# Last groups of a down projection in order of token tiles, the first token tile loaded ahead of a norm's weights, and one power on GpSimd at the beginning

## The chip, the cores and the metric

The kernel runs on one core of one Trainium2 chip. The metric is the device time of one launch in microseconds (us). Engines are named as the profile names them: PE (TensorE), PEld (its weight loads), DVE (VectorE), ACT (ScalarE), POOL (GpSimd) and SP (SyncE, which issues all DMAs of this kernel). Lines are named L275 and the like, by the kernel before.

## The reference, cut to what matters

One decoder layer on x of 512 tokens by 1024 columns, in float32:

```
x = x + 1/2 * SwiGLU_1(RMSNorm(x))
h = RMSNorm(x);  [q | k | v | r | k_r | v_r | c] = h @ W_in
mix = concat(DilatedAttn(QKNorm(q), QKNorm(k), v), RWKV7(r, k_r, v_r, c))
x = x + mix @ W_out
x = x + 1/2 * SwiGLU_2(RMSNorm(x))

SwiGLU(h) = (silu(h @ w_gate) * (h @ w_up)) @ w_down      # 1024 -> 2816 -> 1024
RMSNorm(x) = x * rsqrt(mean(x * x) + 1e-6) * gain
```

## The kernel before

**Tiles.** The 512 tokens are four tiles of 128 (tile 0 to tile 3), the 1024 columns of x two halves of 512 (c = 0, 1). Every float32 product is made as three matmuls of halves of the numbers (`mm3`: high by high, high by low, low by high). So each weight and each transposed x is split into a high part, which ACT casts, and a low part, which DVE or POOL subtracts.

**Stages.** FFN 1 (gate and up projections, then the down projection), the mixing part (W_in, attention, RWKV-7), the W_out projection, FFN 2. The kernel is written with a tile library that orders the instructions of each engine by when they should be ready, in favour of those written first; instructions marked `keep_in_program_order` keep their place. Buffers come from pools with a fixed number of slots; a tile that finds no free slot waits until everything that touches the older one is done.

**The down projection** (`down`) works by a scheme with seven products, m1 to m7, in place of eight: the rows are split in two halves (r = 0 for tiles 0 and 1, r = 1 for tiles 2 and 3), the columns in two, and the 22 blocks of the inner dimension are 11 groups of two. Each product has two accumulators in PSUM (t = 0, 1). `add(acc, t, r, c, sign)` on DVE (L275) adds accumulator t to columns c of tile 2r + t. The last three products are m4, m2 and m6: m4 goes to column half 0 of all four tiles, m2 to both halves of tiles 2 and 3, m6 to half 1 of tiles 2 and 3. Their last three groups (8, 9 and 10) are held back, and `finish(i, m, t)` issues them for one accumulator: nine matmuls of 512 columns. So tile t is complete after m4 of t, and tile 2 + t after m4, m2 and m6 of t.

**The norm that follows.** In FFN 1 a complete tile goes to `done1`, which stores it to DRAM (L471) and calls `norm_T`: the sum of squares of the half that came last (ACT, L96), the scale (POOL, a multiply and add in L115 and a power of -1/2 in L116), the product by scale and gain (DVE, L118, into the tile `xn`, a pool of two slots), and a function, returned, that transposes eight blocks on PE (L125, into two PSUM tiles of the tag "tp", which has two slots) and splits the result into high (ACT, L130) and low (DVE, L131). The transposes are kept in their place of the program. What `down` returns is `hook`, the transposes that are still to be issued; `proj_into` puts them into the first projection of the mixing part, which works on the token columns in two halves of 256 (tiles 0 and 1, then tiles 2 and 3). In FFN 2 nothing follows: `done` returns None, and finished pieces are stored to the output (L277).

Before the change the order is: m4 of t = 0, 1, m2 of t = 0, 1, m6 of t = 0, 1. The transposes of tile 0 stand after m2 of t = 0, those of tile 1 after m2 of t = 1, and those of tiles 2 and 3 are left to `hook`.

**The beginning.** SP's queue holds, in this order, the row of the norm's weights (`row`), tile 0 of x, the identity for transposes, tile 1 of x, then the first two gate and up weights. PE spreads the row over the partitions by matmuls with a row of ones (L457, `one` set on POOL), into two PSUM tiles, `g1`, which DVE multiplies by in L118.

Of the kernel before, what the change touches and what calls it, by code (L numbers as in the profile page):

```python
# [14 lines left out]
ALU = mybir.AluOpType  # L15
# [6 lines left out]
S = 512  # L22
NT = S // P
# [19 lines left out]
def tile_layer(ctx: ExitStack, tc: tile.TileContext, I, out):  # L43
    nc = tc.nc
    V, A, G, T, Q = nc.vector, nc.scalar, nc.gpsimd, nc.tensor, nc.sync
# [10 lines left out]
    nhalf = cpool.tile([P, 16], F32, name="nhalf")[:, 0:8]  # L56
    vec = cpool.tile([P, NV + 2], F32, name="vec")
    fill = spool.tile([P, 24], F32, tag="fill", bufs=1, name="fill")
    G.memset(fill, 0.0)
    G.memset(nhalf, -0.5)  # L60

    def weights(src, width, name, extra=None, lo_eng=None):
        raw = wpool.tile([P, D], F32, tag="wraw", bufs=3, name=f"raw_{name}")
        Q.dma_start(out=raw, in_=src)
        wp = extra or wpool
        hi = wp.tile([P, D], F32R, tag="whi", bufs=2, name=f"hi_{name}")
        lo = wp.tile([P, D], F32R, tag="wlo", bufs=2, name=f"lo_{name}")
        A.copy(out=hi, in_=raw)  # L68
        (lo_eng or V).tensor_tensor(out=lo, in0=raw, in1=hi.bitcast(F32), op=ALU.subtract)  # L69
        return hi.rearrange("p (a b) -> p a b", b=width), lo.rearrange("p (a b) -> p a b", b=width)  # L70
# [8 lines left out]
    def new_xT(name, pool=tpool):  # L79
        return [[pool.tile([P, 4, S], F32R, tag="xT", name=f"{name}{kh}{p}") for p in "hl"] for kh in range(2)]  # L80

    state = {}

    def gain_tile(name):
        g = npool.tile([P, D], F32, tag="gain", bufs=1, name=f"gain_{name}")
        Q.dma_start(out=g, in_=I[name].broadcast_to([P, D]))
        return g[:, 0:S], g[:, S:D]

    def sumsq(x, h, dump, name, eng=None):

        xh = x[:, h * S:(h + 1) * S]
        ss = spool.tile([P, 1], F32, tag="ss", name=f"ss{name}{h}")
        if eng is V:
            V.tensor_tensor_reduce(out=dump, in0=xh, in1=xh, op0=ALU.mult, op1=ALU.add, scale=1.0, scalar=0.0, accum_out=ss)
        else:
            A.activation(out=dump, in_=xh, func=AF.Square, accum_out=ss)  # L96
        return ss

    def guard(ss, name):
        ms = spool.tile([P, 1], F32, tag="ms", bufs=8, name=f"ms{name}")  # L100
        G.tensor_scalar(out=ms, in0=ss, scalar1=1.0 / D, scalar2=EPS, op0=ALU.mult, op1=ALU.add)
        return ms
# [131 lines left out]
    def down(n, U, VV, LL, x, ptile, xp, extra, sd, s17, done, dump, store):  # L234
# [35 lines left out]
        final = set()  # L270

        def add(acc, t, r, c, sign):
            tt = 2 * r + t
            xs = x[tt][:, c * S:(c + 1) * S]
            V.scalar_tensor_tensor(out=xs, in0=acc[t], scalar=0.5 * sign, in1=xs, op0=ALU.mult, op1=ALU.add)  # L275
            if (tt, c) in final and store:
                Q.dma_start(out=store[tt][:, c * S:(c + 1) * S], in_=xs)  # L277
# [27 lines left out]
        ms = [None] * NT  # L305
# [56 lines left out]
        def finish(i, m, t):  # L362
            for g, z in held:
                prod(m, g, *z[i], ts=(t,))

        nxt = [None] * NT
        final.update((tt, c) for tt in range(NT) for c in range(2))
        for t in range(2):
            finish(0, m4, t)
            add(m4, t, 0, 0, 1)  # L370
            nxt[t] = done(t, ms[t])
        final.difference_update([(2, 0), (3, 0), (2, 1), (3, 1)])
        for t in range(2):
            add(m4, t, 1, 0, 1)
        for t in range(2):
            finish(1, m2, t)
            final.add((2 + t, 0))
            add(m2, t, 1, 0, 1)
            add(m2, t, 1, 1, -1)
            if dump:  # L380
                ms[2 + t] = guard(sumsq(x[2 + t], 0, dump(), f"d{n}{2 + t}"), f"d{n}{2 + t}"), 1
            if nxt[t]:
                nxt[t]()
                state.pop('pin', None)
        for t in range(2):
            finish(2, m6, t)
            final.add((2 + t, 1))
            add(m6, t, 1, 1, 1)
            nxt[2 + t] = done(2 + t, ms[2 + t])
        return nxt[2:]  # L390

    def ffn(n, xT, x, hpool, ptile, xp, extra, hook, done, w0, store):
        U, VV, LL, big = [], [], [], []
# [39 lines left out]
    def psum_tiles(c, n, bufs=6):  # L433
        pm = c.enter_context(tc.tile_pool(name=f"pm{n}", bufs=bufs, space=PSUM, reuse_waits="tile"))
        pt = c.enter_context(tc.tile_pool(name=f"pt{n}", bufs=2, space=PSUM, reuse_waits="tile"))
        state['tp'] = lambda shape, tag, name: (pm if tag == "mm" else pt).tile(shape, F32, tag=tag, name=name)
        return state['tp']
# [3 lines left out]
    with ExitStack() as c:  # L441
        xpool = c.enter_context(tc.tile_pool(name="x1", bufs=1, reuse_waits="tile"))
        hpool = c.enter_context(tc.tile_pool(name="h1", bufs=1, reuse_waits="tile"))
        extra = c.enter_context(tc.tile_pool(name="e1", bufs=1, reuse_waits="tile"))
        ptile = psum_tiles(c, 1)
        x1 = [xpool.tile([P, D], F32, name=f"x1_{tt}") for tt in range(NT)]
        xT = new_xT("xa")
        one = spool.tile([1, P], F32, tag="ao", bufs=2, name="one")
        G.memset(one, 1.0)
        row = npool.tile([1, D], F32, tag="gain", bufs=1, name="row")  # L450
        Q.dma_start(out=row, in_=I['ffn1_norm'])
        Q.dma_start(out=x1[0], in_=I['x'][0])
        Q.dma_start(out=ident, in_=I['cst'][:, C_ID:C_ID + P])
        Q.dma_start(out=x1[1], in_=I['x'][1])
        g1 = [ptile([P, S], "mm", f"g1{h}") for h in range(2)]
        for h in range(2):
            T.matmul(g1[h], one, row[:, h * S:(h + 1) * S], start=True, stop=True)  # L457
        for tt in range(2):
            norm_T(x1[tt], g1, xT, tt, "a", tag="tp" if tt == 0 else "mm")()
        w0 = [weights(I['ffn1_w_gu'][0, gu], P, f"gu1_0_{gu}", lo_eng=G) for gu in range(2)]  # L460
        e = state['e']
        for tt in range(2, NT):
            Q.dma_start(out=x1[tt], in_=I['x'][tt])
        with tc.issue_after(e[0].ins), tc.issue_after(e[1].ins):
            hook = [norm_T(x1[tt], g1, xT, tt, "a") for tt in range(2, NT)]

        def done1(tt, ms):
            if tt == 0:
                state['g'] = gain_tile('mix_norm')
                state['xT'] = new_xT("xb")  # L470
            Q.dma_start(out=xd[tt], in_=x1[tt])  # L471
            return norm_T(x1[tt], state['g'], state['xT'], tt, "b", ms)

        hook = ffn(1, xT, x1, hpool, ptile, tpool, extra, hook, done1, w0, None)
# [807 lines left out]
```

## Time and profile before

| | us |
|---|---|
| three runs | 1110.94, 1110.76, 1106.01 (median 1110.76) |
| profiled execution, own time | 1105.09 |
| its span, first to last instruction | 1103.3 |
| PE busy | 1070.1 (97%) |
| DVE, ACT, POOL busy | 677.4, 447.6, 140.5 |

The profile's times count from the start of the span, which is 1.79 us shorter than the execution's own time. PE is busy in almost every slice, so a gain has to come from a stretch in which PE stands, and a loss from one in which it is made to. FFN 1 passes to the mixing part at about 350 to 375 us; the down projection of FFN 2 ends the span.

### The profile page before, as it was taken

How to read it: one execution, taken by the hardware profiler on the slowest of the kernel's cores; microseconds unless marked ns; L12 is line 12 of the kernel's file. 1: busy time of each engine (PE TensorE's matmuls, PEld its weight loads, DVE VectorE, ACT ScalarE, POOL GpSimd, SP SyncE). 2: the span in 40 equal slices, each digit the busy share in tenths (PEclk: the TensorE clock that was granted, in tenths of full speed). 3: DMA queues.
4: the chain of work that ended last, by engine and by line, in shares of the span. 5: the costliest groups of instructions: out<-in, count | busy, mean ns of one | idle time of the engine just before them, and what ended most of it. 6: DMA issues, size and time to landing. Idle time of an engine off the chain costs nothing.

```text
span 1103.3 us, 14413 instructions
## 1 busy us (share of the span) xinstructions
PE 1070.1 (97%) x5380; PEld 896.0 (81%) x5380; DVE 677.4 (61%) x1169; ACT 447.6 (41%) x720; POOL 140.5 (13%) x185
## 2 busy tenths in 40 slices
PE   7999999999999999998899999999999999999998
PEld 6888888888888877777788898788888888888887
DVE  5555464557875735695478468645454655557865
ACT  3332222335654557523343544434332322236652
POOL 3000000000000456203242221212000000000000
PEclk9999999999999999998999999999999999999999
DMA  6556655667556614542321201333566566566663
GB/s 213 181 184 226 227 180 195 225 217 246 189 186 222 200 59 106 153 134 77 105 75 51 86 30 29 129 101 115 194 232 203 181 217 213 199 232 210 212 206 123
DMA packets 84536, 181.14 MB, mean 164 GB/s; under 512 B 23889, under 2 KB 29265, under 8 KB 84466
## 3 DMA queue, kind: packets, MB, share of 16 engines
q1 hardware_dynamic: 84466, 180.22, 50.2%
q8 instruction: 42, 0.69, 0.3%
q14 instruction: 28, 0.23, 0.1%
HBM read 140.87 MB, written 38.27 MB: 162 GB/s over the span
## 4 chain that ended last, share of the span: by engine, by line
PE 79%; DVE 9%; ACT 4%; POOL 3%; DMA 3%; issue 2%; SPq 0%; ACTq 0%; POOLq 0%; DVEq 0%
PE gu L77 14%; PE gu L73 14%; PE gu L76 14%; PE m L76 5%; PE m L77 5%; PE m L73 5%; PE in L77 2%; PE in L76 2%; PE in L73 2%; DMA raw_d<-sd 1%; PE aa L1065 1%; PE cn L1108 1%; DVE pr L867 1%; PE cx L1091 1%; PE acco L76 1%
## 5 line engine op out<-in xcount | busy, mean ns | idle before, releaser
L68 ACT CAST hi_gu<-raw_gu 128x1024 fp32r<-128x1024 f32 x88 | 92.8, 1054 | 271.4 <-PE gu L76 252.3
L69 DVE TENSOR_TENSOR lo_gu<-raw_gu,hi_gu 128x1024 fp32r<-128x1024 f32 x84 | 102.5, 1220 | 49.9 <-ACT hi_gu L68 49.9
L405 DVE TENSOR_TENSOR sg<-gu,sg 128x512 f32<-128x512 f32 x44 | 30.3, 688 | 68.4 <-PE gu L77 67.6
L76 PE MATMUL gu<-xc0l,hi_gu 128*128 128x512 f32 (+1 forms) x184 | 70.0, 380 | 1.6 <-DVE xc0l L131 1.6
L73 PE MATMUL gu<-xa0h,hi_gu 128*128 128x512 f32 (+1 forms) x184 | 70.7, 384 | 0.7 <-ACT xa0h L130 0.7
L76 PE MATMUL gu<-xa0l,hi_gu 128*128 128x512 f32 (+1 forms) x184 | 70.5, 383 | 0.4 <-DVE xa0l L131 0.4
L77 PE MATMUL gu<-xa0h,lo_gu 128*128 128x512 f32 (+1 forms) x184 | 70.4, 383 | 0.0
L73 PE MATMUL gu<-xc0h,hi_gu 128*128 128x512 f32 (+1 forms) x184 | 70.0, 380 | 0.0
L73 PE MATMUL gu<-xa1h,hi_gu 128*128 128x512 f32 (+1 forms) x184 | 70.0, 380 | 0.0
L73 PE MATMUL gu<-xc1h,hi_gu 128*128 128x512 f32 (+1 forms) x184 | 70.0, 380 | 0.0
L77 PE MATMUL gu<-xc1h,lo_gu 128*128 128x512 f32 (+1 forms) x184 | 69.9, 380 | 0.0
L76 PE MATMUL gu<-xc1l,hi_gu 128*128 128x512 f32 (+1 forms) x184 | 69.9, 380 | 0.0
L76 PE MATMUL gu<-xa1l,hi_gu 128*128 128x512 f32 (+1 forms) x184 | 69.9, 380 | 0.0
L77 PE MATMUL gu<-xc0h,lo_gu 128*128 128x512 f32 (+1 forms) x184 | 69.9, 380 | 0.0
L77 PE MATMUL gu<-xa1h,lo_gu 128*128 128x512 f32 (+1 forms) x184 | 69.9, 380 | 0.0
L259 DVE TENSOR_TENSOR lo_d<-raw_d,hi_d 128x1024 fp32r<-128x1024 f32 x39 | 47.6, 1224 | 17.7 <-ACT hi_d L258 17.5
L76 PE MATMUL m<-lo_d,v 128*128 128x512 f32 x148 | 57.7, 390 | 0.2 <-DVE lo_d L259 0.2
L73 PE MATMUL m<-hi_d,v 128*128 128x512 f32 x148 | 57.7, 390 | 0.0
L77 PE MATMUL m<-hi_d,l 128*128 128x512 f32 x140 | 54.5, 389 | 0.0
L259 DVE TENSOR_TENSOR w_d<-raw_d,w_d 128x1024 fp32r<-128x1024 f32 x35 | 42.7, 1222 | 16.1 <-ACT w_d L258 16.0
L231 ACT CAST v<-u 128x512 fp32r<-128x512 f32 (+1 forms) x58 | 33.0, 570 | 45.5 <-PE m L76 45.4
L73 PE MATMUL m<-w_d,v 128*128 128x512 f32 x132 | 51.3, 389 | 0.0
(388 smaller groups left out, 2651.6 us busy)
## 6 DMA issues: line engine op xcount, KB each, us to landing
raw_gu<-in_ffn_w_gu SPq DMA_DIRECT2D x88, 512.0 KB, 4.1
raw_d<-sd SPq DMA_DIRECT2D x66, 256.0 KB, 3.5
raw_in<-in_w_in SPq DMA_DIRECT2D x28, 512.0 KB, 3.7
ra<-in_ffn_w_down SPq DMA_DIRECT2D x22, 512.0 KB, 3.5
rb<-in_ffn_w_down SPq DMA_DIRECT2D x22, 512.0 KB, 5.3
sd<-s SPq DMA_DIRECT2D x22, 512.0 KB, 5.2
s<-ra SPq DMA_DIRECT2D x22, 512.0 KB, 6.0
raw_d<-in_ffn_w_down SPq DMA_DIRECT2D x44, 256.0 KB, 3.3
```

The source lines that it names most:

```text
L68: A.copy(out=hi, in_=raw)
L69: (lo_eng or V).tensor_tensor(out=lo, in0=raw, in1=hi.bitcast(F32), op=ALU.subtract)
L73: first = T.matmul(ps, lh, rh, start=start, stop=False)
L76: T.matmul(ps, lh, rl, start=False, stop=False)
L77: T.matmul(ps, ll, rh, start=False, stop=stop)
L231: A.copy(out=hi, in_=src)
L259: V.tensor_tensor(out=lo, in0=raw, in1=hi.bitcast(F32), op=ALU.subtract)
L405: V.tensor_tensor(out=sg, in0=ps[1], in1=sg, op=ALU.mult)
L867: V.tensor_tensor(out=pr[:, :n1, :n2], in0=au[:, i + 1:, i:i + 1].broadcast_to([P, n1, n2]), in1=tu[:, i:i + 1, :n2].broadcast_to([P, n1, ...
L1065: T.matmul(ps[:, c], bk[:, j, c], xr[:, j, c, 2 * h:2 * h + 2], start=True, stop=True)
L1091: T.matmul(px[:, j, h], xr[:, j, c, 2 * h:2 * h + 2].rearrange("p a b -> p (a b)"), sv[:, j, h, c, :], start=True, stop=True)
L1108: T.matmul(pn[:, j, h], kr[:, j, c, 2 * h:2 * h + 2].rearrange("p a b -> p (a b)"), sv[:, j, h, c, :], start=True, stop=True)
```

## The change

Three parts. In the last groups of `down`, everything of t = 0 is issued first (m4, m2, m6), then everything of t = 1; so the tiles are complete in the order 0, 2, 1, 3. The functions with the transposes go into a list, `late`, from which `turned(n)` issues the oldest until n are left: those of tiles 0 and 2 after m2 of t = 1, those of tile 1 after m6 of t = 1; those of tile 3 alone are returned as `hook`. At the beginning, tile 0 of x is put ahead of the row of weights in SP's queue. And POOL does one power, of a tile of ones, before anything else but two memsets.

```diff
-    G.memset(fill, 0.0)
+    G.memset(fill, 1.0)
     G.memset(nhalf, -0.5)
+    G.tensor_tensor(out=fill[:, 0:8], in0=fill[:, 8:16], in1=nhalf, op=ALU.pow)
...
         nxt = [None] * NT
-        final.update((tt, c) for tt in range(NT) for c in range(2))
+        late = []
+
+        def closed(tt, c):
+
+            if store:
+                Q.dma_start(out=store[tt][:, c * S:(c + 1) * S], in_=x[tt][:, c * S:(c + 1) * S])
+
+        def turned(n):
+            while len(late) > n:
+                f = late.pop(0)
+                if f:
+                    f()
+                    state.pop('pin', None)
+
         for t in range(2):
             finish(0, m4, t)
             add(m4, t, 0, 0, 1)
-            nxt[t] = done(t, ms[t])
-        final.difference_update([(2, 0), (3, 0), (2, 1), (3, 1)])
-        for t in range(2):
+            closed(t, 0)
+            late.append(done(t, ms[t]))
             add(m4, t, 1, 0, 1)
-        for t in range(2):
             finish(1, m2, t)
-            final.add((2 + t, 0))
+            turned(2 - t)
             add(m2, t, 1, 0, 1)
+            closed(2 + t, 0)
             add(m2, t, 1, 1, -1)
             if dump:
                 ms[2 + t] = guard(sumsq(x[2 + t], 0, dump(), f"d{n}{2 + t}"), f"d{n}{2 + t}"), 1
-            if nxt[t]:
-                nxt[t]()
-                state.pop('pin', None)
-        for t in range(2):
             finish(2, m6, t)
-            final.add((2 + t, 1))
+            turned(1)
             add(m6, t, 1, 1, 1)
-            nxt[2 + t] = done(2 + t, ms[2 + t])
-        return nxt[2:]
+            closed(2 + t, 1)
+            late.append(done(2 + t, ms[2 + t]))
+        turned(1)
+        return late
...
+        Q.dma_start(out=x1[0], in_=I['x'][0])
         Q.dma_start(out=row, in_=I['ffn1_norm'])
-        Q.dma_start(out=x1[0], in_=I['x'][0])
```

## Rows read from the trace of the kernel before

**Rows 1.** Waits of PE from 345 to 382 us: total, times, longest.
```profile
PE pTb L125 <- DVE xb0l L131: 1.5, 2, 1.2
```
**Rows 2.** Timeline of PE, FFN 1 to mixing: start, duration, instruction, idle before.
```profile
355.69 0.39 PE L73 MATMUL m<-hi_d,v 128*128 128x512 f32 x1
...
357.74 1.04 PE L125 MATMUL pTb<-ident,xnb 128*128 128x128 f32 x8
358.53 0.47 PE L73 MATMUL m<-hi_d,v 128*128 128x512 f32 x1
...
362.96 0.66 PE L125 MATMUL pTb<-ident,xnb 128*128 128x128 f32 x4 [1.23 <-DVE xb0l L131]
...
367.27 0.27 PE L76 MATMUL in<-xb0l,hi_in 128*128 128x256 f32 x1
...
372.80 1.25 PE L125 MATMUL pTb<-ident,xnb 128*128 128x128 f32 x8 [0.31 <-DVE xb0l L131]
```
**Rows 3.** Timeline of DVE, the same stretch.
```profile
356.42 1.42 DVE L118 SCALAR_TENSOR_TENSOR xnb<-x,rsb,gain_mix_norm 128x512 f32<-128x512 f32 x2 [1.32 <-POOL rsb L116]
...
362.23 0.68 DVE L131 TENSOR_TENSOR xb0l<-pTb,xb0h 128x512 fp32r<-128x512 f32 x1
```
**Rows 4.** Timeline of ACT, the same stretch.
```profile
354.60 0.63 ACT L96 ACTIVATE xnb<-x 128x512 f32<-128x512 f32 x1 [2.87 <-DVE x L275]
...
359.16 0.57 ACT L130 CAST xb0h<-pTb 128x512 fp32r<-128x512 f32 x1
...
360.36 1.03 ACT L68 CAST hi_in<-raw_in 128x1024 fp32r<-128x1024 f32 x1
```
**Rows 5.** Timeline of POOL, the same stretch.
```profile
355.49 0.26 POOL L115 TENSOR_SCALAR rsb<-ssb,msd 128x1 f32<-128x1 f32 x1 [61.55 <-ACT xnb L96]
355.84 0.55 POOL L116 TENSOR_TENSOR rsb<-rsb,nhalf 128x1 f32<-128x1 f32 x1
...
361.47 4.82 POOL L69 TENSOR_TENSOR lo_in<-raw_in,hi_in 128x1024 fp32r<-128x1024 f32 x2 [0.38 <-ACT hi_in L68]
```
**Rows 6.** Timeline of all engines at the beginning.
```profile
0.72 0.35 SPq L451 DMA_DIRECT2D row<-in_ffn_norm  x1
...
2.25 3.75 PE L457 MATMUL g<-row,one 1*128 1x512 f32 x4 [2.25 <-DMA row<-in_ffn_norm]
...
4.71 0.69 DVE L94 CUSTOM_DVE_ANT_0 xna<-x 128x512 f32<-128x512 f32 x1 [4.71 <-DMA x<-in_x]
...
6.16 0.56 POOL L116 TENSOR_TENSOR rsa<-rsa,nhalf 128x1 f32<-128x1 f32 x1
...
6.61 0.69 DVE L94 CUSTOM_DVE_ANT_0 xna<-x 128x512 f32<-128x512 f32 x1 [1.20 <-DMA x<-in_x]
...
7.23 2.83 DVE L118 SCALAR_TENSOR_TENSOR xna<-x,rsa,g 128x512 f32<-128x512 f32 x4
...
8.89 1.05 ACT L68 CAST hi_gu<-raw_gu 128x1024 fp32r<-128x1024 f32 x1 [1.56 <-DMA raw_gu<-in_ffn_w_gu]
...
10.01 4.73 POOL L69 TENSOR_TENSOR lo_gu<-raw_gu,hi_gu 128x1024 fp32r<-128x1024 f32 x2 [1.40 <-ACT hi_gu L68]
...
17.86 1.67 PE L125 MATMUL pTa<-ident,xna 128*128 128x128 f32 x8 [1.62 <-DVE xna L118]
```
**Rows 7.** Timeline of the end of the span.
```profile
1099.54 0.69 DVE L275 SCALAR_TENSOR_TENSOR x<-m,x 128x512 f32<-128x512 f32 x1 [1.35 <-PE m L77]
1100.26 0.33 SPq L277 DMA_DIRECT2D out_y<-x  x1
```
**Rows 8.** Timeline of PE at the opening of FFN 2.
```profile
760.38 0.39 PE L76 MATMUL gu<-xc0l,hi_gu 128*128 128x256 f32 x1 [1.55 <-DVE xc0l L131]
```
**Rows 9.** Stretches: length, busy time of PE, PEld, DVE, ACT, POOL, granted clock, DMA.
```profile
20.00:22.00 2.00, 2.00 (x11) 2.00 (x11) 0.89 (x2) 0.16 (x1) 0.40 (x3) 0.50 0.69 188
...
362.00:365.00 3.00, 2.04 (x13) 1.81 (x14) 2.87 (x6) 2.01 (x4) 3.00 (x2) 1.00 0.11 11
```
**Rows 10.** Instructions of L1135, powers on POOL: minimum, median, maximum ns.
```profile
L1135 POOL TENSOR_TENSOR gw<-gw,nhalf x4: 1636/1641/2659, 579.3 to 701.1; 128x8 f32<-128x8 f32 x4
```

## Prediction

> **What bounds the kernel now.** I read the table of busy times first: PE works 97% of the span, so what this change can move is found where PE stands, in the three stretches that it touches. The list of PE's waits for the passage from FFN 1 to the mixing part names one cause only, the transposes `pTb`, which waited twice, 1.5 us in all [rows 1]. The timeline of PE shows both places: 1.23 us in front of the transposes of tile 1, whose PSUM slot was still being read for tile 0's low part on DVE until 362.91, and 0.31 us in front of those of tile 3 [rows 2, 3]. These 1.54 us are all the standing that the passage has to give. The timelines of ACT and POOL then show what a late tile passes through [rows 4, 5]. At the beginning the timeline of all engines shows which queue is last: PE stands for 1.62 us in front of 17.86 us because POOL subtracts low parts of weights from 10.01 to 14.74 and only then comes to the scales of tiles 2 and 3 [rows 6]. At the end of the span nothing stands between the last product, its addition and its store [rows 7].
>
> **The change part by part.**
>
> *The end (FFN 2).* Nothing follows here, so the new order only permutes PE's nine-matmul blocks and the output stores. The last block is m6 of t = 1 in both orders, and its addition (1099.54) and store (1100.26) are the end [rows 7]. The store issued just before it belongs to tile 3, half 0, where it was tile 2, half 1; both are one block, 2.05 us, earlier. A block is 357.74 - 355.69 = 2.05 us [rows 2] and makes at most two additions of 0.69 us [rows 7], so DVE keeps up. 0 us.
>
> *The passage, PE alone.* Up to 355.69 us the two orders cost PE the same: two blocks done. In the new order m6 of t = 0 begins there, m4 of t = 1 at 357.74, m2 of t = 1 at 359.79, and the transposes of tile 0 at 361.84. Eight transposes take 358.53 - 357.74 = 0.79 us [rows 2]. With m6 of t = 1 (2.05) and the transposes of tile 2 (0.79), those of tile 1 could begin at 365.47. They come directly before the first projection, which reads them. From their start to the first matmul that needs a low part it takes half the transposes (0.40), a cast on ACT (0.57), a subtraction on DVE (0.68) [rows 2 to 4] and, an estimate from the gaps in these rows, 0.2 us for three hand-overs: 1.85 us, so 367.3 at best. In the trace that matmul stands at 367.27 [rows 2]. But then only tile 3 is left for `hook`; the trace still pays 0.79 us for the transposes of tile 2 and the 0.31 us behind. So the new order is even with the old one when this matmul starts at 367.27 + 0.79 + 0.31 = 368.37.
>
> *What is late next.* Three tiles now wait for transposes where two did: `norm_T` of tile 1 is called while tiles 0 and 2 still hold the two slots of `xn`. Its sum of squares on ACT writes into that tile, so it waits until PE has transposed tile 0, at 361.84 + 0.79 = 362.63. Behind it in ACT's queue stand the casts of the first weights of the mixing part, and behind those the two subtractions of L69 on POOL; POOL's queue also makes the scale of tile 1, for which DVE and then PE wait. From the start of the sum to POOL's first step took 355.49 - 354.60 = 0.89 us [rows 4, 5], which gives 363.52; POOL's two steps take 0.90 us and the first half of the product 0.75 (half of 1.42 and a hand-over of 0.04) [rows 3, 5]. The first of L69 started 361.47 - 358.53 = 2.94 us after m2 of t = 1 began, because its buffers are then free [rows 2, 5]; in the new order that is 359.79 + 2.94 = 362.73, and each lasts 4.82 / 2 = 2.41 us. So the scale of tile 1 comes in a queue that has just become busy. Three orders are possible there:
>
> - the scale first: it ends at 364.42, tile 1 is ready in time, the matmul stands at 367.3: 1.1 us gained;
> - one subtraction ahead, to 365.14: scale until 366.04, transposes from 366.8, matmul at 368.7: 0.3 us lost;
> - both ahead, to 367.55: scale until 368.45, transposes from 369.2, matmul at 371.1: 2.7 us lost.
>
> I take the middle one: the first subtraction is ready 0.8 us before the scale, the second cannot start before 365.14, when the scale has long been ready. The nearest place that already runs like this, the opening of FFN 2, where PE waits for a low part made from fresh transposes, stood 1.55 us [rows 8], which is within these bounds. Tile 3 follows after m6 of t = 1; its place is 36 matmuls of 256 columns into the projection, some 4 us later, and hides its chain of about 4 us.
>
> What the clock does in such a gap: the trace shows the granted clock at 1.00 (2.4 GHz) through the 1.23 us stand [rows 9], and at 0.50 (1.2 GHz) in 20 to 22 us, some 2 us after PE stood 1.62 us at the beginning [rows 6, 9]. Two us at half clock lose about 1 us of work. I count none, since the middle case stands for about 1.3 us and then some 1 us, with eight transposes between. The Trainium skill, TensorE: Matmul & The Clock Gate, section "Why this matters for your kernels", advises against idle gaps between bursts of matmuls, since the engine falls back to half rate; for this change, which puts a stand where PE flowed on, it would add about that 1 us. The stand of 1.23 us in this same stretch did not do it.
>
> *The row behind tile 0.* Tile 0 gains the place of one issue, about 0.4 us in SP's queue (the row's 0.35 us and a gap) [rows 6]. Its scale was ready at 6.72, but DVE multiplied from 7.23, since the sum of tile 1, which landed at 6.61, stands in between; tile 1 keeps its place behind the same bytes. So nothing starts earlier. The row is later: not less than by 0.4 us (2.65), not more than to the landing of tile 0 in the old order (4.71). PE spreads it in 3.75 us, so `g1` is complete between 6.4 and 8.5 us, against a need for its second half at about 7.9. At worst 0.6 us late; it lies under the cast of weights on ACT (to 9.94) and POOL's subtractions (to 14.74), which set PE's stand at 17.86 [rows 6]. 0 us; 0.6 lost without that cover.
>
> *The power.* 128 x 8 elements take 1.64 us [rows 10], at POOL's start. Behind it in POOL's queue stands only `one`, 1.6 us later than before, at about 2.6 us, and PE's spreading waits for it: no later than the row above. POOL is then idle until tile 0 has landed. Does it take something away later? The first power of the trace lasts 0.56 us, at 6.16; one in the passage, 0.55 [rows 5, 6]. No first-time cost is there to remove. 0 us.
>
> **Sum.** 0 + 0.3 + 0 + 0 = 0.3 us lost. Against the profiled execution that is 1105.09 + 0.3 = 1105.4. But the median of the runs, 1110.76, lies 5.67 us above that execution, and the lowest run, 1106.01, near it; the spread of one kernel is larger than anything summed here. A time is most likely near the median shown: 1110.76 + 0.3 = 1111.1.
>
> **The rivals.**
>
> *A, the gap does not form* (1.1 us gained: 1109.7). For it: the scale is a short step and was written first, so a queue ordered by readiness may keep POOL for it. Against it: 0.8 us of idle POOL would have to be left for it.
>
> *B, both subtractions ahead of the scale* (2.7 us lost: 1113.5). For it: in the trace POOL does both in one stretch, from 361.47 to 366.29 [rows 5]. Against it: the new scale is ready before the second starts.
>
> *C, slower: ACT stands at the sum of tile 1.* Issued as soon as m4 of t = 1 is added (about 360.7), it holds ACT until 362.63; the cast in front of L69, due at 361.6, moves to about 363.4, both subtractions by 1.8 us, the second to 369.3; a scale behind them ends at 370.2, the matmul stands at 372.9: 4.5 us lost. One more cast (1.03 us, [rows 4]) in front makes it 5.5: 1116.3. It decides from a scale that ends after 371.2.
>
> *D, the first power hides a price.* The Trainium skill, GPSIMD Engine Reference, section "Instruction dispatch", gives the first call of a freshly loaded kernel on GpSimd about 6 us that no instruction shows; the sum by it would be up to 6 us lower. In these rows such a price would have to lie ahead of 6.72, where the first scale ends, and even a scale at once could not start DVE before 7.23. It would have to sit in the launch; by the rows at most the 1.79 us outside the span could go: 1111.1 - 1.8 = 1109.3.
>
> **How the numbers follow.** The middle case 0.50, A 0.22, B 0.17, C 0.05, D 0.02, and 0.04 for orders of queues elsewhere that the new tracing shifts. Predicted 1111.1. The range goes from A on the lowest run, 1106.01 - 1.1 = 1104.9, to B on the highest, 1110.94 + 2.7 = 1113.6. A measurement of this kernel can tell about 0.5% (5.6 us) from no change. Same: 0.86, which holds the middle case, A, B and D except where the spread carries them out. Faster: 0.08, from the 0.5 us by which A on the lowest run passes 1105.2. Slower: 0.06, C and the rest.
>
> **What would show it.** In the profile after: PE's waits in the passage name L131's `xb0l` in front of the first `in` matmul, at 368 to 369 us; ACT's sum of tile 1 is released by PE's transposes of tile 0; POOL has one subtraction of L69, the scale, then the other. At the beginning PE's stand in front of 17.9 us is unchanged and `g` starts between 2.6 and 4.8. The end keeps its distances. Wrong would be: no wait for `xb0l` (A), 4.82 us of L69 in one piece ahead of the scale (B), ACT standing before its casts (C), a first power that is much longer than 1.64 us (D).

## The result and the profile after

The changed kernel takes 1115.53 us (median of 9 runs, 1112.6 to 1118.2), the kernel before 1106.93 us in the runs beside it (9 runs, 1097.88 to 1110.94): ratio 1.0087, 95% interval 1.0065 to 1.0109. It is slower by about 0.9%, where 1111.1 us and no measurable change were predicted, and it lies above the predicted range.

The profiled execution after took 1115.53 us, with a span of 1113.7 us, 10.4 us more than before. I locate the loss with one measure, the **stretch** from the first addition of m4 on DVE to the first 512-column product of the mixing part on PE; PE has the same work in it in both kernels. These are its two ends in the timelines, first before, then after:

```profile
353.81 1.29 DVE L275 SCALAR_TENSOR_TENSOR x<-m,x 128x512 f32<-128x512 f32 x2 [0.82 <-PE m L77]
...
381.08 0.40 PE L73 MATMUL in<-xb0h,hi_in 128*128 128x512 f32 x1
```

```profile
353.50 1.29 DVE L276 SCALAR_TENSOR_TENSOR x<-m,x 128x512 f32<-128x512 f32 x2 [0.82 <-PE m L78]
...
390.71 0.40 PE L74 MATMUL in<-xb0h,hi_in 128*128 128x512 f32 x1
```

27.27 us became 37.21: 9.94 us of the 10.4 are lost here. PE's waits in the passage after (total, times, longest) answer to [rows 1]:

```profile
PE pTb L126 <- DVE xb0l L132: 6.5, 2, 5.9
PE in L77 <- DVE xb0l L132: 1.3, 1, 1.3
```

PE stands for 7.8 us where it stood for 1.5. The three timelines show why, PE's first (it answers to [rows 2]):

```profile
361.49 1.04 PE L126 MATMUL pTb<-ident,xnb 128*128 128x128 f32 x8
...
370.50 1.94 PE L126 MATMUL pTb<-ident,xnb 128*128 128x128 f32 x8 [5.92 <-DVE xb0l L132]
372.99 1.97 PE L126 MATMUL pTb<-ident,xnb 128*128 128x128 f32 x8 [0.55 <-DVE xb0l L132]
...
376.86 0.58 PE L77 MATMUL in<-xb0l,hi_in 128*128 128x256 f32 x1 [1.28 <-DVE xb0l L132]
...
378.09 0.41 PE L74 MATMUL in<-xb0h,hi_in 128*128 128x256 f32 x1
378.30 0.41 PE L77 MATMUL in<-xb0l,hi_in 128*128 128x256 f32 x1
```

The three sets of transposes are those of tiles 0, 2 and 1. Tile 0's are in time; tile 2's, which the prediction put directly behind m6 of t = 1 (at 364.68), stand for 5.92 us. They need the two PSUM slots that tile 0's low parts on DVE still read. DVE (as [rows 3]):

```profile
361.45 1.42 DVE L119 SCALAR_TENSOR_TENSOR xnb<-x,rsb,gain_mix_norm 128x512 f32<-128x512 f32 x2 [1.92 <-POOL rsb L117]
362.78 2.68 DVE L276 SCALAR_TENSOR_TENSOR x<-m,x 128x512 f32<-128x512 f32 x4
368.34 1.41 DVE L119 SCALAR_TENSOR_TENSOR xnb<-x,rsb,gain_mix_norm 128x512 f32<-128x512 f32 x2 [2.88 <-POOL rsb L117]
369.67 0.68 DVE L132 TENSOR_TENSOR xb0l<-pTb,xb0h 128x512 fp32r<-128x512 f32 x1
370.27 0.68 DVE L132 TENSOR_TENSOR xb1l<-pTb,xb1h 128x512 fp32r<-128x512 f32 x1
```

DVE idles for 2.88 us in front of tile 1's product, which waits for its scale, and tile 0's low parts stand behind that product in DVE's queue. The first two lines are tile 2's product and the four additions behind it, of which the first completes tile 1. POOL (as [rows 5]):

```profile
362.17 5.26 POOL L70 TENSOR_TENSOR lo_in<-raw_in,hi_in 128x1024 fp32r<-128x1024 f32 x2 [0.75 <-ACT hi_in L69]
367.41 0.27 POOL L116 TENSOR_SCALAR rsb<-ssb,msd 128x1 f32<-128x1 f32 x1
367.76 0.55 POOL L117 TENSOR_TENSOR rsb<-rsb,nhalf 128x1 f32<-128x1 f32 x1
```

Both subtractions are ahead of tile 1's scale, in one stretch: rival B's order. ACT (as [rows 4]):

```profile
361.05 2.00 ACT L69 CAST hi_in<-raw_in 128x1024 fp32r<-128x1024 f32 x2 [0.70 <-ACT xnb L97]
363.58 0.63 ACT L97 ACTIVATE xnb<-x 128x512 f32<-128x512 f32 x1 [0.54 <-DVE x L276]
```

The sum that the scale needs began at 363.58, released by DVE's addition, and the casts of the first two weights were ahead of it, not behind it; ACT did not stand for tile 0's transposes, so C did not happen.

The stands are 6.2 us of the 9.94. The rest, 3.7 us, goes with the clock. Stretches after (length, PE busy, granted clock, DMA; as [rows 9]):

```profile
360.00:364.00 4.00, 4.00 (x24) 1.00 0.32 131
364.00:368.00 4.00, 0.58 (x3) 0.87 0.74 281
368.00:372.00 4.00, 1.50 (x7) 0.50 0.39 145
372.00:376.00 4.00, 3.03 (x13) 0.50 0.83 252
376.00:380.00 4.00, 3.14 (x14) 0.50 0.80 248
380.00:384.00 4.00, 4.00 (x33) 0.93 0.16 66
```

After the long stand PE works at 1.2 GHz from 368 to past 380 us: eight transposes take 1.94 us instead of 1.04, and the 256-column products start 0.21 us apart, from 380.63 on 0.12. At these distances the sixteen transposes lose about 2 us against the 0.79 us that eight take in the kernel before, and the nineteen products ahead of 380.63 about 1.7 us.

At the beginning, PE's spreading of the row starts at 4.15, tile 1 lands later, and GpSimd's subtractions begin 0.54 us later than in [rows 6]; by 353.50 us the changed kernel is nevertheless 0.31 us ahead. That says little: in the runs below that share this beginning the same addition starts anywhere from 351.66 (e6) to 353.94 (e2). The power lasts 1.65 us:

```profile
0.81 0.20 POOL L460 MEMSET one<- 1x128 f32 x1
1.06 1.65 POOL L61 TENSOR_TENSOR fill<-fill,nhalf 128x8 f32<-128x8 f32 x1
...
4.15 3.75 PE L468 MATMUL g<-row,one 1*128 1x512 f32 x4 [4.15 <-DMA row<-in_ffn_norm]
4.24 0.69 DVE L95 CUSTOM_DVE_ANT_0 xna<-x 128x512 f32<-128x512 f32 x1 [4.24 <-DMA x<-in_x]
...
8.11 0.69 DVE L95 CUSTOM_DVE_ANT_0 xna<-x 128x512 f32<-128x512 f32 x1 [3.17 <-DMA x<-in_x]
...
10.55 4.69 POOL L70 TENSOR_TENSOR lo_gu<-raw_gu,hi_gu 128x1024 fp32r<-128x1024 f32 x2 [0.44 <-ACT hi_gu L69]
```

At the end of the span the last addition (as [rows 7]) starts 3.76 us ahead of the end, as before:

```profile
1109.94 0.69 DVE L276 SCALAR_TENSOR_TENSOR x<-m,x 128x512 f32<-128x512 f32 x1 [0.75 <-PE m L78]
```

### The profile page after: what moved, and what is told of

Same layout as the page of the kernel before. It is cut to its first block, busy times and chain, and to the rows that moved or that the text cites. A ratio compares the mean times of both kernels' runs of the same rounds, so it can differ in the third digit from the quotient of the medians.

```text
span 1113.7 us, 14413 instructions
## 1 busy us (share of the span) xinstructions
PE 1073.3 (96%) x5380; PEld 897.4 (81%) x5380; DVE 675.7 (61%) x1169; ACT 447.5 (40%) x720; POOL 142.2 (13%) x186
## 4 chain that ended last, share of the span: by engine, by line
PE 79%; DVE 9%; ACT 3%; POOL 3%; issue 3%; DMA 2%; ACTq 0%; SPq 0%; POOLq 0%; DVEq 0%
PE gu L78 14%; PE gu L77 14%; PE gu L74 14%; PE m L77 5%; PE m L74 5%; PE m L78 5%; PE in L77 3%; PE in L78 3%; PE in L74 3%; DMA raw_d<-sd 1%; PE aa L1076 1%; PE po L1000 1%; PE cn L1119 1%; PE acco L77 1%; PE acco L78 1%
## 5 line engine op out<-in xcount | busy, mean ns | idle before, releaser
L416 DVE TENSOR_TENSOR sg<-gu,sg 128x512 f32<-128x512 f32 x44 | 30.2, 687 | 68.4 <-PE gu L78 67.6
L213 DVE TENSOR_TENSOR s<-ra 128x512 f32<-128x512 f32 x22 | 15.2, 693 | 59.9 <-DMA ra<-in_ffn_w_down 59.9
```

Source lines behind the costliest of these rows:

```text
L213: V.tensor_tensor(out=t[:, 1], in0=ra[:, 1], in1=ra[:, 0], op=ALU.subtract)
L416: V.tensor_tensor(out=sg, in0=ps[1], in1=sg, op=ALU.mult)
```

## The experiments

All ratios are to the kernel before on the same chip, in up to five rounds. Stretch and PE's stands in it are those of one profiled execution; "rest" is the stretch less 27.27, less the stands over 1.5.

| run | what it is | stretch | stands | rest | ratio (95%) |
|---|---|---|---|---|---|
| before | | 27.27 | 1.5 | 0 | 1 |
| after | the change | 37.21 | 7.8 | 3.7 | 1.0087 (1.0065 to 1.0109) |
| e1 | order alone | 38.01 | 7.8 | 4.5 | 1.0106 (1.0053 to 1.0159) |
| e5 | beginning alone | 27.27 | 1.6 | 0 | 0.9993 (0.9972 to 1.0015) |
| e2 | low parts of weights on DVE | 32.46 | 4.1 | 2.6 | 1.0060 (1.0031 to 1.0089) |
| e3 | tile 0's transposes early | 30.27 | 2.5 | 2.0 | 1.0025 (1.0000 to 1.0050) |
| e4 | PE filled with 25 matmuls | 34.95 | 2.9 | 0.5 | 1.0090 (1.0063 to 1.0117) |
| e6 | products behind low parts | 32.46 | 4.0 | 2.7 | 1.0061 (1.0037 to 1.0086) |
| e7 | e6 and e2 | 32.50 | 4.0 | 2.7 | 1.0028 (1.0002 to 1.0055) |
| e8 | e3 and e2 | 32.19 | 2.9 | 3.5 | 1.0048 (1.0025 to 1.0072) |
| e9 | scale first on GpSimd | 38.24 | 9.4 | 3.1 | 1.0109 (1.0081 to 1.0138) |
| e10 | e6, one subtraction ahead | 32.24 | 3.8 | 2.7 | 1.0048 (1.0023 to 1.0073) |
| e11 | e6, none ahead | 33.81 | 5.4 | 2.6 | 1.0073 (1.0050 to 1.0096) |
| e12 | e3, e6 and e9 | 30.16 | 2.6 | 1.8 | 1.0041 (1.0020 to 1.0063) |
| e13 | e9 with memsets | 31.70 | 3.5 | 2.4 | 1.0022 (0.9997 to 1.0047) |
| e14 | e12 with memsets | 29.02 | 2.3 | 1.0 | 1.0034 (1.0009 to 1.0059) |

In e4 the rest also leaves out 5.83 us of added matmuls. In every row the stretch alone accounts for the time: (stretch - 27.27) / 1105 lies inside the interval of the ratio, from 0.00% in e5 to 0.99% in e9. Many of these intervals overlap, so the runs are told apart by their traces more than by their times; the two traces of the same order, of the change and of e1, differ by 0.8 us of stretch.

**Which part.** e1 has only the new order, e5 only the two edits of the beginning.

```diff
 e1, from the change:
-    G.tensor_tensor(out=fill[:, 0:8], in0=fill[:, 8:16], in1=nhalf, op=ALU.pow)
...
-        Q.dma_start(out=x1[0], in_=I['x'][0])
         Q.dma_start(out=row, in_=I['ffn1_norm'])
+        Q.dma_start(out=x1[0], in_=I['x'][0])
 e5: these edits the other way, in the kernel before
```

> The change without its two parts at the beginning: only the new order of the last groups. My theory: the whole loss is made in the passage from FFN 1 to the mixing part, by the queue of GpSimd, which has both subtractions of L69 ahead of the scale of tile 1. Then the ratio to before is 1.008 to 1.010, the stretch from the first addition of m4 to the first 512-column matmul of the mixing part is 37 us (27.3 in before), and PE stands about 6 us in front of the transposes of tile 2. Rival 1, the beginning costs it: ratio 0.998 to 1.002, stretch 27 to 29 us.

> The kernel before with only the two edits of the beginning: tile 0 of x ahead of the row of weights, and the power of a tile of ones on GpSimd. The order of the last groups is that of before. My account of the beginning: 0 us, ratio 0.998 to 1.002, since the stand of PE at 17.9 us hangs on GpSimd's subtractions and not on the row. In the profiled changed kernel the first addition of m4 came 0.31 us earlier, so a gain of some 0.3 us would still fit. Rival (the beginning carries a part of the loss, as the second tile landed at 8.11 us instead of 6.61): ratio 1.003 or more, and the first addition of m4 1 us or more later than 353.8.

Both much as my theory had it: the order alone costs 1.06% (a little above the range that I gave, with a stand of 5.9 us and a stretch of 38.0), the beginning nothing that can be told from zero: its interval goes from -3.1 to +1.7 us.

**The queue of GpSimd.** e2 takes the first two subtractions away from it.

```diff
-    proj_into(accs, [weights(I['w_in'][24 + ct], P, f"in6_{ct}", lo_eng=G) for ct in range(2)], xT, hook)
+    proj_into(accs, [weights(I['w_in'][24 + ct], P, f"in6_{ct}") for ct in range(2)], xT, hook)
```

> The whole change, but DVE instead of GpSimd subtracts the low parts of the first two weights of the mixing part, so that nothing long stands in GpSimd's queue ahead of the scale of tile 1; the order of DVE (product of tile 1 ahead of the low parts of tile 0) and of PE's transposes is as in the change. My theory (GpSimd's queue): the scale of tile 1 comes within 1.5 us of its sum, PE's stand in front of the transposes of tile 2 falls from 5.9 us to under 2, the clock stays at 1.00, the stretch is 27 to 30 us, ratio 0.998 to 1.004. Rival 2, the two PSUM slots and three tiles in flight make the stand whatever GpSimd does: stand 4 us or more, ratio 1.006 or more.

Between the two: the stand in front of tile 2's transposes falls from 5.9 to 3.6 us, not below 2, and the stretch to 32.5. The ratio, 1.0060, reaches the 1.006 that rival 2 asked for, and its interval overlaps that of the change. DVE and PE in e2:

```profile
366.43 1.42 DVE L119 SCALAR_TENSOR_TENSOR xnb<-x,rsb,gain_mix_norm 128x512 f32<-128x512 f32 x2 [0.20 <-POOL rsb L117]
367.76 0.68 DVE L132 TENSOR_TENSOR xb0l<-pTb,xb0h 128x512 fp32r<-128x512 f32 x1
```

```profile
368.59 1.94 PE L126 MATMUL pTb<-ident,xnb 128*128 128x128 f32 x8 [3.58 <-DVE xb0l L132]
```

Tile 1's product now starts at 366.43, but tile 0's low parts still come behind it, at 367.76. So a late scale is one link, and DVE's order seems to be another; e6 tries that one.

**The order of the transposes.** e3 issues tile 0's one block earlier, behind m6 of t = 0, so that its low parts are made (358.50) before any later product is due.

```diff
             finish(2, m6, t)
-            turned(1)
+            turned(t)
```

> The whole change, but the transposes of tile 0 are issued after m6 of t = 0 instead of after m2 of t = 1, so that at most two tiles wait for transposes. GpSimd's program then has one subtraction ahead of the scale of tile 1, the other behind it. My theory: the stand in front of the transposes of tile 2 is gone (under 1 us), what is left is a stand of 1 to 2 us behind those of tile 1; stretch 26.5 to 29 us, clock 1.00, ratio 0.997 to 1.003. Rival 3, the last transposes directly before the projection that reads them cost the time: stretch 32 us or more, ratio 1.005 or more.

The ratio held; stand (2.5), stretch (30.3) and clock (0.57 from 368 to 372 us) missed. DVE and PE in e3:

```profile
365.40 1.41 DVE L119 SCALAR_TENSOR_TENSOR xnb<-x,rsb,gain_mix_norm 128x512 f32<-128x512 f32 x2 [0.72 <-POOL rsb L117]
366.74 0.68 DVE L132 TENSOR_TENSOR xb0l<-pTb,xb0h 128x512 fp32r<-128x512 f32 x1
```

```profile
367.47 1.34 PE L126 MATMUL pTb<-ident,xnb 128*128 128x128 f32 x8 [2.51 <-DVE xb0l L132]
```

The same link appears one tile later, tile 2's low parts (366.74) behind tile 1's product (365.40), and PE stands for 2.5 us in front of tile 1's transposes.

**The clock.** e4 keeps PE busy in the place of the 5.9 us stand with matmuls that nothing reads; the queues of the other engines are as in the change.

```diff
-            turned(2 - t)
+            ...                   # for t = 1 only tile 0's transposes; tile 2's behind the added matmuls
...
             finish(2, m6, t)
+            if n == 1 and t == 1:
+                d = ptile([P, S], "mm", "fillps")
+                (v1, _), (h1, _) = held[0][1][0]
+                for _ in range(25):
+                    tc.keep_in_program_order(T.matmul(d, v1[:, 0:P], h1, start=True, stop=True))
```

> The whole change, with 25 more matmuls of 512 columns on PE, results unused, between m6 of t = 1 and the transposes of tile 2: they fill the stand of 5.9 us and change no wait. They leave the queues of GpSimd, DVE and ACT in the order of the change. If the half clock after the stand costs about 4 us of the loss: granted clock 1.00 to the transposes, sixteen transposes in 1.6 us instead of 3.9, stretch 33 to 34 us, ratio 1.004 to 1.006. If the clock costs nothing: stretch 37 us, ratio 1.008 or more.

Its stretches (columns as above) stay at 2.4 GHz:

```profile
368.00:372.00 4.00, 3.37 (x18) 1.00 0.45 136
372.00:376.00 4.00, 1.76 (x10) 1.00 0.94 313
376.00:380.00 4.00, 3.90 (x32) 1.00 0.99 279
```

The stretch fell by 2.3 us, not by 3 to 4, because at full clock PE stood longer for low parts (1.8 us in front of the products). The time did not fall: 1.0090 is a ratio that I had given for a clock that costs nothing. The 0.70% that its stretch gives is inside the interval; whether the rest is chance or a cost elsewhere stays open. What the clock costs is thus read from traces; no time shows it.

**DVE's order.** e6 puts tile 1's product behind tile 0's low parts, and tile 3's behind tile 1's; GpSimd's queue stays as in the change. e7 moves the two subtractions to DVE as well.

```diff
-        for h in range(2):
-            V.scalar_tensor_tensor(...)
+        def product(): ...
+        if name == 'b' and tt % 2:
+            state['product'] = product
...
+            if name == 'b' and tt < 2:
+                state['low'] = state['e'][1]
...
             turned(2 - t)
+            if 'product' in state:
+                with tc.issue_after(state.pop('low').ins):
+                    state.pop('product')()
```

> The changed kernel, but on DVE the product of tile 1 is written behind tile 0's low parts, and that of tile 3 behind tile 1's. GpSimd's queue is unchanged: both subtractions stay ahead of tile 1's scale. My theory (the loss has two links, the late scale of tile 1 behind two subtractions, and DVE's queue, which holds tile 0's low parts and so two PSUM slots behind the product that waits for that scale): with the second link cut, what is left is the case that the prediction priced at 2.7 us. The stand of PE in front of tile 2's transposes falls from 5.9 us to 2 or less, the first matmul that needs a low part comes near 371 us instead of 376.9, the stretch from the first addition of m4 to the first 512-column product of the mixing part is 29.5 to 33 us (37.2 in the changed kernel, 27.3 in the kernel before), ratio 1.002 to 1.006. Rival (GpSimd's two subtractions alone make the loss, whatever DVE's order): stretch 35 us or more, ratio 1.008 or more.

> The same order on DVE, and the first two subtractions of the mixing part's weights moved from GpSimd to DVE, so that tile 1's scale waits for nothing on GpSimd. My theory: both links are cut; no stand in front of tile 2's transposes above 2 us, low parts wanted near 369 us, stretch 27.5 to 30.5 us, ratio 0.999 to 1.003. Rival (the loss comes from the order of the blocks itself, from tiles that become complete too late whatever the queues do): stretch 32 us or more, ratio 1.005 or more.

PE's waits in e6:

```profile
PE pTb L131 <- DVE xb0l L137: 1.5, 1, 1.5
PE pTb L131 <- DVE xnb L120: 1.2, 1, 1.2
PE in L74 <- ACT xb0h L136: 0.7, 1, 0.7
PE pTb L131 <- DVE xb1l L137: 0.6, 1, 0.6
```

The 5.9 us stand is gone and the stands add up to 4.0, that is 2.5 more than before. The prediction had priced rival B at 2.7, but put it all in front of tile 1's transposes; here those wait 1.2 us, and 2.1 us are still in front of and within tile 2's, for tile 0's low parts. The ratio, 1.0061, is just above what I gave, since the rest, with the clock at 0.50 from 368 to 372 us, adds 2.7 us. e7 missed its stretch (32.5, not below 30.5, and so that of its rival), though the ratio is in its range: on DVE the first weight's low part (1.21 us at 362.79) now delays the addition that completes tile 2's half and tile 0's low parts, so PE stands 2.5 us there instead.

**Both links, from the early side.** e8 joins e3 and e2.

```diff
-            turned(1)
+            turned(t)
...
-    ... f"in6_{ct}", lo_eng=G) ...
+    ... f"in6_{ct}") ...
```

> The changed kernel with tile 0's transposes behind m6 of t = 0, one block earlier than in the change, and the first two subtractions on DVE. With the transposes early alone 2.5 us of stand were left in front of tile 1's transposes, since tile 2's low parts then stood behind the product of tile 1, whose scale waited for one subtraction (to 364.5 us). Without that subtraction on GpSimd the scale can start some 0.9 us earlier. My theory: stand 1 to 2 us, stretch 27.5 to 30 us, ratio 0.997 to 1.003; if any arrangement of the new order beats the kernel before, it is this one. Rival (something else holds tile 1 or tile 2): stand 2.5 us or more, stretch 30 us or more, ratio 1.003 or more.

Missed: stretch 32.2, ratio 1.0048. The stand in front of tile 1 fell to 1.7 us, but the first product that needs a weight's low part then stood 0.99 us for DVE. The subtraction is a cost on either engine.

**The prediction's three cases.** e9 puts the scale first on GpSimd and leaves DVE's order as in the change. e11 and e10 have e6's order on DVE with none and one subtraction ahead of the scale (e6 is the same with two).

```diff
-        (lo_eng or V).tensor_tensor(out=lo, in0=raw, in1=hi.bitcast(F32), op=ALU.subtract)
+        if name in ('in6_0', 'in6_1'):        # e10: ('in6_1',)
+            with tc.issue_after(state['scale'].ins):
+                lo_eng.tensor_tensor(out=lo, in0=raw, in1=hi.bitcast(F32), op=ALU.subtract)
...
-        G.tensor_tensor(out=rs, in0=rs, in1=nhalf[:, 0:1], op=ALU.pow)
+        p = G.tensor_tensor(out=rs, in0=rs, in1=nhalf[:, 0:1], op=ALU.pow)
+        if name == 'b' and tt == 1:
+            state['scale'] = p
```

> The changed kernel with one thing else: on GpSimd the first two subtractions of the mixing part's weights are written behind the scale of tile 1, so the scale comes first (the case that the prediction called A in GpSimd's queue). DVE's order is as in the change: the product of tile 1 ahead of tile 0's low parts. My theory (two links): the scale ends near 365.3 us instead of 368.3, the product at 366.6, tile 0's low parts follow, so PE still stands about 2.8 us in front of tile 2's transposes; stretch from the first addition of m4 to the first 512-column product 30.5 to 32.5 us (27.3 before, 37.2 in the change), ratio 1.003 to 1.006. Rival (GpSimd's queue is all of it): stretch under 29 us, ratio under 1.002. Rival (GpSimd's queue is nothing of it): stretch 36 us or more, ratio 1.008 or more.

> On DVE the product of tile 1 is written behind tile 0's low parts and that of tile 3 behind tile 1's, as in the earlier run of that order; on GpSimd one subtraction ahead of the scale of tile 1 and one behind it. This is the prediction's middle case, which it priced at 0.3 us lost. With two ahead the stretch was 32.5 us, of it 4.0 us of stands and 2.7 us of half clock. By my theory one subtraction less takes away the stand of 1.24 us in front of tile 1's transposes, but not the 2.1 us in front of and within tile 2's, which hang on tile 0's low parts: stretch 30 to 32 us, ratio 1.003 to 1.005. Rival (the prediction's price holds once the order is the predicted one): stretch 27 to 28.5 us, ratio 0.999 to 1.001.

> The same order on DVE, and on GpSimd the scale of tile 1 ahead of both subtractions: the prediction's case A, which it priced at 1.1 us gained. My theory: no better than with one ahead, since then the scale is no longer what comes last; stretch within 1 us of the run with one ahead (30 to 32 us), ratio 1.002 to 1.005. Rival (A's price holds): stretch 25.5 to 27.5 us, ratio below 1.000.

e9 missed my theory and looked like its second rival: 1.0109, a stand of 7.1 us. But its timelines show another cause. POOL and DVE in e9:

```profile
364.53 5.09 POOL L72 TENSOR_TENSOR lo_in<-raw_in,hi_in 128x1024 fp32r<-128x1024 f32 x2
```

```profile
364.63 5.53 DVE L125 SCALAR_TENSOR_TENSOR xnb<-x,rsb,gain_mix_norm 128x512 f32<-128x512 f32 x2
370.09 0.68 DVE L138 TENSOR_TENSOR xb0l<-pTb,xb0h 128x512 fp32r<-128x512 f32 x1
```

The scale was ready and the product started at 364.63, 3.7 us earlier than in the change, but its two halves took 5.53 us instead of 1.41. Each half ended some 0.5 us behind one of the two subtractions (the second of these began at 366.83). e10 has the ratio that I gave and a stretch (32.2) just above it, but the stand in front of tile 1's transposes, which I had taken away, is still 1.0 us. e11 missed both ranges and is worse than e10 by 1.6 us, for the reason seen in e9: its first half product took 2.44 us (367.30 to 369.74) while both subtractions ran to 369.19. So with one subtraction ahead 2.3 us of stands are lost, not 0.3, and with none ahead nothing is gained.

**What held the product.** e12 joins e3, e6 and e9. e13 is e9, and e14 is e12, with memsets on GpSimd in the place of the two subtractions.

```diff
 e12, with e6's and e9's edits:
-            if name == 'b' and tt < 2:
+            if name == 'b' and tt:
...
-            turned(1)
+            turned(t)
 e13, e14:
-                lo_eng.tensor_tensor(out=lo, in0=raw, in1=hi.bitcast(F32), op=ALU.subtract)
+                for _ in range(3):
+                    lo_eng.memset(lo.bitcast(F32), 0.0)
```

> All three together: tile 0's transposes behind m6 of t = 0, on GpSimd the scale of tile 1 ahead of both subtractions, and on DVE each product behind the low parts that free the PSUM slots. With the early transposes alone the stretch was 30.3 us, with 2.5 us of stand and about 2 us of half clock. My theory: about 1.2 us of stand is left in front of tile 1's transposes, and with a stand that short the clock does not fall or falls for less; stretch 27 to 29.5 us, ratio 0.998 to 1.002. If it is under 26.5 us with a ratio below 0.998, the new order can beat the kernel before; if it is above 30 us, something that I have not named holds tile 1.

> The kernel with the scale of tile 1 first on GpSimd (e9), with three memsets of each low part in the place of the subtraction that makes it, so that GpSimd is as busy behind the scale but reads nothing from SBUF. It leaves out the low parts of the first two weights of the mixing part (they are zero). In e9 each half of tile 1's product on DVE took 2.8 us beside a subtraction on GpSimd, where it takes 0.75 alone, while additions and low parts, which read one operand from PSUM, kept their 0.69 us. My theory (the product reads both operands from SBUF and is held while GpSimd's subtraction, which also does, runs): the halves take 0.75 us here, PE's stand in front of tile 2's transposes falls from 7.1 us to 2 to 3.5, the stretch from 38.2 us to 31 to 33, ratio 1.003 to 1.006. Rival (a busy GpSimd holds DVE whatever it runs, or the trace only shows the product wrongly): halves above 2 us, stand 5 us or more, ratio 1.008 or more.

> The kernel with all three changes (e12: tile 0's transposes behind m6 of t = 0, the scale of tile 1 first, each product behind the low parts), with the same memsets in the place of the first two subtractions; the low parts of two weights are left out (zero). In e12 the product of tile 1 took 2.26 us for its halves in place of 1.41, and PE stood 2.6 us for it. My theory: 1.41 us, a stand of 1 to 2 us, stretch 27.5 to 29.5 us (e12: 30.2), ratio 0.999 to 1.003, so that the new order is at best even with the old one even without the subtractions. Rival (the new order pays once nothing is in its way): stretch under 27 us and a ratio below 0.999.

e12 missed: stretch 30.2, ratio 1.0041, with the product at 2.26 us and a stand of 2.6 us behind it. That was the "something that I have not named". e13 names it; POOL and DVE:

```profile
365.33 1.85 POOL L73 MEMSET lo_in<- 128x1024 f32 x2
367.26 0.19 POOL L107 TENSOR_SCALAR msd<-ssd 128x1 f32<-128x1 f32 x1
367.51 3.63 POOL L73 MEMSET lo_in<- 128x1024 f32 x4
```

```profile
365.44 1.40 DVE L126 SCALAR_TENSOR_TENSOR xnb<-x,rsb,gain_mix_norm 128x512 f32<-128x512 f32 x2
366.77 0.68 DVE L139 TENSOR_TENSOR xb0l<-pTb,xb0h 128x512 fp32r<-128x512 f32 x1
```

Beside a memset the product takes its 1.40 us, the stand falls to 2.97 us and the stretch to 31.7; the ratio, 1.0022, is a little better than I gave. GpSimd is as busy as in e9, but reads nothing. e14 had its stand (1.8) and stretch (29.0) as expected, at full clock throughout; its ratio, 1.0034, is just above what I gave. Even without the subtractions the new order does not beat the old one, and no run here was measurably faster than the kernel before.

## Why the prediction was wrong

**Right:** the end (0 us: the distances are the same), the power (1.65 us, nothing behind it), that rival C and rival D would not happen (for D, the time outside the span is 1.8 us before and after), and the place of the loss.

**Right by luck:** the beginning. Its 0 us lies in e5's interval, but not by the way that was predicted. "Tile 1 keeps its place behind the same bytes" is not borne out: with the row behind tile 0 the sum of tile 1 started at 8.11 us in the change, and between 6.62 (e14) and 8.01 (e2) in the other runs; with the row ahead, at 6.61 (before) and 7.46 (e1). `one` was set ahead of the power, at 0.81, not behind it. The first gate and up product started at 14.25 instead of 12.39, and the stand that was to stay unchanged at 17.86 was 0.79 us at 18.95. Cover is not all that made up for this: from 20 to 22 us the kernel before had a clock of 0.50 [rows 9] and the changed one 1.00. e1, with the beginning of the kernel before, had 1.00 there too, so it is not the order that decides this. (A slip besides: from 1104.9 to 1105.2 it is 0.3 us, not the 0.5 in "Faster".) By luck, too, the time is no further off than 4.4 us: the 1110.76 from which it was counted lies 3.8 us above the median of the runs beside the change, 1106.93.

**The step that failed:** "I take the middle one: the first subtraction is ready 0.8 us before the scale, the second cannot start before 365.14, when the scale has long been ready." The reasoning orders GpSimd's queue by when its work is ready in the trace. But that order is fixed before the kernel runs, by the tile library, and there both subtractions stand first, although the scale is written ahead of them: its sum ended at 364.30, the second subtraction began at 365.08 all the same, and the scale waited for it until 367.41. In e10, where only the order on GpSimd differs from e6, the scale runs between the two, at 364.30. Why the library put them so stays open. The scale's end, 368.31, is what rival B had worked out (368.45). The passage's term, 0.3 us, measured 9.94: 6.2 us of stands and 3.7 us that go with the clock.

**The link that was missing in all three cases:** "those of tile 1 could begin at 365.47" lets tile 2's transposes run directly behind m6 of t = 1. They need the PSUM slots of tile 0, which DVE frees, and DVE's queue held that release behind the product that waited for the late scale. So a late scale of tile 1 stopped tile 2 first. B with the missing link is 6.2 us of stands, not 2.7. e6, in which the product no longer stands ahead of that release, has 2.5, but 2.1 us of its stands still wait for the same slots, so that the sum comes near 2.7 is luck. The prices of the other two cases missed too: with one subtraction ahead the stands grow by 2.3 us (e10, 0.3 predicted), with none by 3.9 (e11, 1.1 gained predicted), and in e11 the stand in front of tile 1's transposes is 1.6 us longer than in e10 by the product that was held beside GpSimd (below). DVE's queue delayed the sum of tile 1 as well: the addition that completes that tile stood behind tile 2's product, which had waited 1.92 us for its own scale, so the sum began at 363.58 and not at 362.63.

**The clock:** "I count none" was wrong by 3.7 us in the change. The rule of the Trainium skill that the prediction weighed there (TensorE: Matmul & The Clock Gate, "Why this matters for your kernels") agrees with this trace: 0.50 from 368 to 380 us, behind a stand of 5.92 us. The traces of e4 and e14 fit that size: the clock stayed at 1.00 and the rest was 0.5 and 1.0 us, where the other runs of the new order have 1.8 to 4.5. The length of a single stand does not tell whether the clock falls: 1.62 us at the beginning of the kernel before was followed by 0.50, 1.76 us in e14 and 1.78 us in e4 by 1.00.

**What the prediction left out:** the product held beside GpSimd (e9, 5.53 us for 1.41; e13, 1.40). The Trainium skill, SBUF — State Buffer, section "Who interferes with whom", says that a DVE instruction with two inputs in SBUF contends with a GpSimd instruction that reads SBUF, and not with one that only writes it. The runs agree in both halves. DVE's additions and low parts, with one input in PSUM, kept 0.69 us beside the subtractions.

My own theory of two links, with which the experiments began, was incomplete too: cutting both (e7, e8) left 0.3 to 0.5%. The chain from a finished tile to its PSUM slots being free passes additions and sums of other tiles on DVE and ACT, and PE stands for part of it in every arrangement of the new order that was tried. What the smallest possible stand of this order is stays open.

## What to carry to other kernels

Where a change moves a step into a stretch with other work, write down the order of each queue that the step passes, as the built program has it (it need not be the order of the source), and ask of every instruction behind a waiting one what it would have freed: here a scale on GpSimd stopped, through DVE's queue, the PSUM slots of another tile. A stand of PE costs more than its length when the clock falls behind it; read the granted clock of the stretch with the waits. Work given to GpSimd is not always off DVE's way: here a product of DVE with both tensors in SBUF was held while a subtraction on GpSimd ran. A trace shows this as an instruction that lasts longer than the same shape elsewhere, not as a wait.

## What the runs showed of the hardware

- Each half of the product of 128x512, with both tensors in SBUF, lasted 2.8 us beside a 128x1024 subtraction on GpSimd (e9) and 0.75 alone or beside a memset (e13); the subtraction lasted 2.94 us where the product had started first (e10, 361.36), and the next one 2.36.
- The granted clock stood at 0.50 for about 12 us after a stand of 5.92 us and shorter ones behind it; in e14 it stayed at 1.00 after a stand of 1.76 us; in the kernel before it was at 0.50 from 20 to 22 us after one of 1.62 us, in e1 at 1.00 there after one of 1.31.
- When a tile lands differs between executions by more than this change of order can be seen to move it: the sum of tile 1 started between 6.62 and 8.11 us with the row behind tile 0 (14 runs), and at 6.61 and 7.46 with the row ahead (2 runs).
